# Nine of eleven feed-forward parts projected down by threes, as seven block products in place of eight

## The chip, the cores and the metric

The kernel runs on one core of a Trainium2 chip. Times are device microseconds of one execution, and the number that counts is their median. A core has TensorE (matrix products, written PE in the profile, its weight loads PEld), VectorE (DVE), ScalarE (ACT), GpSimd (POOL) and SyncE (SP), which here issues the loads. TensorE writes only to PSUM, eight banks of 512 fp32 columns; VectorE and ScalarE read and write PSUM, GpSimd does not.

## The reference, cut to what matters

Two sequences of 256 and 512 tokens go through a network of two layers, each a mixer and a feed-forward stage, with a normalisation before each. Weights are shared, and the kernel takes the two sequences side by side as 768 columns. The stage that is changed is this one, in both layers:

```python
def conv_ffn(h, w_up, conv_w, conv_b, w_down):
    u = h @ w_up                                  # 1024 -> 2 x 2816
    u = conv_general_dilated(u, conv_w, ...) + conv_b   # width 3, along the tokens
    g = u[..., :D_FF]
    val = u[..., D_FF:]
    return (jax.nn.silu(g) * val) @ w_down        # 2816 -> 1024
x = x + g2 * conv_ffn(h, ...)
```

All arrays are fp32. The kernel computes a product of two fp32 matrices with three products of the short type fp32r: each operand is split into a high part and a remainder (high x high, high x low, low x high).

## The kernel before, in words

Channels lie on the 128 partitions and tokens along the free axis, so that x is kept as eight channel chunks of 768 tokens, in two large tiles (`xt`).

The 2816 inner channels are cut into eleven parts of 256, that is two chunks of 128 for the gate and two for the value. `ffn` (L1372) loops over the parts. For each part `up` (L1405) makes:

- two calls of `pair` (L1194), one for the gate and one for the value. A pair is itself a block product by seven: input channel halves, two output chunks and token halves (384 columns) are combined, and `quarters` (L1162) issues twelve matmuls of 128x384 for each of the seven, into four fixed PSUM banks. Its weight blocks are summed on GpSimd (L1202 to L1214), split, and its sums are carried between banks by ScalarE copies (L1218, L1229);
- `conv` (L1384) on each chunk: one ScalarE and two VectorE instructions (L1387 to L1390);
- `silu` on ScalarE, put off into the next pair, and `product` (L1399): gate times value on GpSimd (L1402), then the split into high and low by `fp_copy_split` (L256), whose first line runs on ScalarE (L260) and whose second on VectorE (L261).

`down` (L1441) projects a finished part, while the loop is already at the next one. Its weights come in two loads of 128x1024, each split whole. Then for each output chunk c of eight and each sequence (512 and 256 tokens) it issues two times three matmuls into a PSUM bank of the group called `pa`, of four, and `resid` (L587) adds the result, times a factor, to x on VectorE. A part has 96 such matmuls and 16 such adds.

What sets the order: instructions are traced in program order, and a planner orders those of each engine by priority (earlier in the program first) and by its own estimate of when each is ready, and it inserts the waits. Where a block stands under `manual_schedule` with an engine's name, that engine keeps the program's order there. Outside, the matmuls of a part's down projection are laid between those of the next part's pairs. Each engine then executes its own list strictly in order. All loads go through the queue of SP, in order.

Buffers are handed out by name, and a new tile waits until an old one is no longer read. Those that matter:

```python
def slab(self, shape, dt=F32):   # tag "slab", bufs=6   (large, 12 KB a partition)
def tmp(self, shape, dt=F32):    # tag "nt",   bufs=8   (128x384)
def raw(self, src):              # tag "raw",  bufs=5   (a load, 128x1024)
def split(self, src):            # tags "whi", "wlo", bufs=3 each
```

In the feed-forward stage x holds two slabs, `urows` two (the first only in part 0), and the convolved rows `yrow` and the split product `g` take turns in the rest.

The last two parts, 9 and 10, are followed by the next stage's normalisation; part 0 is started by `head` (L1257), which is written out by hand and overlaps the end of the projection before.

Of the kernel before, what the change touches and what calls it, by code (L numbers as in the profile page):

```python
# [12 lines left out]
R = mybir.dt.float32r  # L13
# [3 lines left out]
P = 128  # L17
# [15 lines left out]
FF = 2816  # L33
FC = FF // P
NPART = FC // 2
EPS = 1e-6
LAG = 3

# [129 lines left out]
class Net:  # L168
# [1025 lines left out]
    def pair(self, pool, u, bank, rows, rest=False, behind=None):  # L1194
# [49 lines left out]
        self.quarters(d, part(wb, 1), self.T4, False)  # L1244
        self.evict(r2, d)

    def prepare(self, u0):
# [124 lines left out]
    def ffn(self, l, xt, pool, last_tile, apply, keep=None):  # L1372
# [22 lines left out]
        def silu(yrow):  # L1395
            for j in range(2):
                nc.scalar.activation(yrow[:, j], yrow[:, j], AF.Silu)

        def product(yrow, g):  # L1399
            for j in range(2):  # L1400
                y = yrow[:, 2 + j]
                nc.gpsimd.tensor_tensor(y, y, yrow[:, j], ALU.mult)  # L1402
                self.fp_copy_split(g[:, 0, j], g[:, 1, j], y)

        def up(p):  # L1405
# [8 lines left out]
            g = self.slab([P, 2, 2, TG], R)  # L1414
            for i in range(2):
                if p:
                    rows = [urow[:, 2 * i + j] for j in range(2)]
                    with ExitStack() as order:
                        for ins in behind[2 * i :] if p == 1 else ():
                            order.enter_context(self.tc.issue_after(ins))  # L1420

                        other = p == i == 1
                        bank = lambda j: self.pa()[:, :H] if j == 1 and other else fixed(j)
                        self.pair(pool, u0 + 3 * p + i, bank, rows, p == 1, held.pop() if held else None)
                for j in range(2):
                    conv(urow[:, 2 * i + j], yrow[:, 2 * i + j], i * FC + 2 * p + j)
                if i == 0:
                    held.append(lambda: silu(yrow))
            if p:
                product(yrow, g)  # L1430
            else:
                gate = held.pop()
                held.append(lambda: (gate(), product(yrow, g)))
            return g

        def mark(t):
# [231 lines left out]
```

## Time and profile before

| | |
|---|---|
| median of 3 runs | 1843.68 us (1842.69 to 1843.8) |
| the profiled execution | 1843.78 us, span 1842.0 us |
| TensorE | 1793.2 us busy, 97% of the span, 11290 matmuls |
| VectorE | 1367.0 us, 74% |
| ScalarE | 895.3 us, 49% |
| GpSimd | 488.0 us, 26% |
| granted clock of TensorE | 0.994 in the mean |
| the feed-forward parts in the steady state | 46.4 us each, TensorE busy throughout |

In the tables a line names the kernel's line, the engine, the operation, the tiles (written <- read), the shape and the count; behind the bar stand busy time and the mean duration of one in ns, then the idle time of the engine just before them and what ended it. The tables by stretch give for each window its length, then busy time and count for TensorE, its weight loads, VectorE, ScalarE and GpSimd, then the granted clock (1.00 is full), the DMA engines' share and GB/s. Rows of the timeline give start, duration and the instruction. Matmuls overlap one another, so that the distance of two starts is the time that one takes, not its own duration.

### The profile page before, as it was taken

The page shows a single profiled execution, that of the slowest core. Times are in us where ns is not written, and L with a number is a line of the kernel's source. Part 1 is how long each engine was busy: PE and PEld are TensorE (multiplying, and loading weights), DVE is VectorE, ACT ScalarE, POOL GpSimd, SP SyncE. Part 2 cuts the span into 40 slices and gives each one's busy share as a digit, 9 for nine tenths or more (in the row PEclk, how much of TensorE's full clock was granted, in tenths as well). Part 3 has the DMA queues.
Part 4 walks back from the last instruction along what each step waited for, and adds up shares of the span by engine and source line. Part 5 has one row for each costly group of instructions (what it writes and reads, how often), then busy time and mean ns, then how long its engine had stood idle before and what let it go on. Part 6 is the DMA issues. An engine that isn't in the chain of part 4 may idle for free.

```text
span 1842.0 us, 28931 instructions
## 1 busy us (share of the span) xinstructions
PE 1793.2 (97%) x11290; PEld 1657.4 (90%) x11290; DVE 1367.0 (74%) x2101; ACT 895.3 (49%) x1815; POOL 488.0 (26%) x386
## 2 busy tenths in 40 slices
PE   6999999999999999999999999999999999999997
PEld 3987887889998999999999999889989999999997
DVE  4755676886689877777777757766898777777776
ACT  4443443354456444444444556765564444444443
POOL 1001001021024333333331313430144333333322
PEclk9999999999999999999999999999999999999999
DMA  8344566546312221222223321124122222222212
GB/s 330 119 145 134 172 195 221 164 138 219 101 46 74 76 61 66 69 69 69 69 69 93 104 83 50 53 94 129 50 86 69 69 69 69 69 69 70 69 35 69
DMA packets 64245, 184.48 MB, mean 100 GB/s; under 512 B 6167, under 2 KB 23831, under 8 KB 64108
## 3 DMA queue, kind: packets, MB, share of 16 engines
q1 hardware_dynamic: 64108, 182.63, 30.8%
q8 instruction: 89, 1.46, 0.3%
q14 instruction: 48, 0.39, 0.1%
HBM read 176.17 MB, written 6.43 MB: 99 GB/s over the span
## 4 chain that ended last, share of the span: by engine, by line
PE 86%; DVE 6%; DMA 3%; ACT 2%; issue 1%; POOL 1%; SPq 0%; POOLq 0%; ACTq 0%; DVEq 0%
PE ps L254 27%; PE pa L254 25%; PE ps L1169 10%; PE ps L1172 10%; PE ps L1170 10%; PE pa L1008 1%; DMA slab<-in_adaln_w_dram 1%; DMA raw<-in_w_dram 1%; DVE wlo L261 1%; DVE ada L506 1%; DVE slab L590 1%; DMA raw<-in_adaln_w_dram 0%; PE pa L1172 0%; PE pa L1169 0%; PE pa L1170 0%
## 5 line engine op out<-in xcount | busy, mean ns | idle before, releaser
L260 ACT CAST whi<-raw 128x1024 fp32r<-128x1024 f32 x237 | 247.9, 1048 | 350.4 <-PE pa L254 161.4
L261 DVE TENSOR_TENSOR wlo<-raw,whi 128x1024 fp32r<-128x1024 f32 x237 | 316.6, 1337 | 119.8 <-ACT whi L260 117.3
L254 PE MATMUL pa<-slab,whi 128*128 128x256 f32 (+1 forms) x1472 | 346.6, 331 | 3.2 <-DVE slab L590 3.2
L254 PEld LDWEIGHTS pa<-slab,whi 128*128 128x128 f32 x1472 | 252.7, 188 | 27.5 <-DVE slab L590 4.5
L590 DVE SCALAR_TENSOR_TENSOR slab<-pa,mod,slab 128x256 f32<-128x256 f32 (+1 forms) x368 | 211.2, 592 | 70.8 <-PE pa L254 70.5
L254 PE MATMUL pa<-slab,wlo 128*128 128x256 f32 (+1 forms) x736 | 233.9, 330 | 0.0
L254 PE MATMUL ps<-zh,whi 128*128 128x256 f32 (+1 forms) x560 | 189.0, 339 | 2.3 <-ACT whi L260 1.7
L254 PE MATMUL ps<-zh,wlo 128*128 128x256 f32 (+1 forms) x560 | 184.1, 330 | 2.0 <-DVE wlo L261 2.0
L254 PE MATMUL ps<-zl,whi 128*128 128x256 f32 (+1 forms) x560 | 185.1, 332 | 0.0
L1169 PE MATMUL ps<-zh,whi 128*128 128x384 f32 x504 | 172.3, 342 | 3.6 <-ACT nt L1240 1.8
L1170 PE MATMUL ps<-zl,whi 128*128 128x384 f32 x504 | 169.9, 337 | 0.8 <-DVE zl L1126 0.8
L1172 PE MATMUL ps<-zh,wlo 128*128 128x384 f32 x504 | 168.9, 335 | 0.0
L254 PEld LDWEIGHTS pa<-slab,wlo 128*128 128x128 f32 x736 | 138.5, 188 | 13.1 <-DVE wlo L261 0.4
L1205 POOL TENSOR_TENSOR raw<-raw,raw 128x512 f32<-128x512 f32 x40 | 52.2, 1305 | 330.8 <-DVE wlo L261 259.4
L254 PE MATMUL ps<-slab,whi 128*128 128x384 f32 x512 | 132.0, 339 | 0.9 <-DVE slab L261 0.5
L1402 POOL TENSOR_TENSOR slab<-slab 128x772 f32<-128x772 f32 x44 | 86.5, 1967 | 164.6 <-DVE slab L1390 152.7
L1389 DVE SCALAR_TENSOR_TENSOR slab<-slab,cstt,slab 128x771 f32<-128x771 f32 x88 | 103.6, 1179 | 26.6 <-ACT slab L1387 26.5
L254 PEld LDWEIGHTS ps<-zh,whi 128*128 128x128 f32 x560 | 107.4, 192 | 15.9 <-issue 4.4
L506 DVE SCALAR_TENSOR_TENSOR ada<-raw,silc,ada 128x1024 f32<-128x1024 f32 x84 | 110.6, 1354 | 14.9 <-DMA raw<-in_adaln_w_dram 14.8
L1202 POOL TENSOR_TENSOR raw<-raw 128x512 f32<-128x512 f32 x40 | 68.5, 1712 | 200.1 <-DMA raw<-in_w_dram 169.7
L254 PEld LDWEIGHTS ps<-zh,wlo 128*128 128x128 f32 x560 | 107.2, 192 | 12.2 <-DVE wlo L261 2.9
L254 PEld LDWEIGHTS ps<-zl,whi 128*128 128x128 f32 x560 | 107.4, 192 | 11.9 <-issue 3.4
(291 smaller groups left out, 4265.7 us busy)
## 6 DMA issues: line engine op xcount, KB each, us to landing
raw<-in_w_dram SPq DMA_DIRECT2D x208, 512.0 KB, 3.7
raw<-in_adaln_w_dram SPq DMA_DIRECT2D x84, 512.0 KB, 4.6
slab<-in_x_dram SPq DMA_DIRECT2D x12, 512.0 KB, 6.8
slab<-in_adaln_w_dram SPq DMA_DIRECT2D x12, 512.0 KB, 10.3
slab<-mrows SPq DMA_DIRECT2D x8, 384.0 KB, 5.3
xs<-slab SPq DMA_DIRECT2D x6, 512.0 KB, 3.6
bt<-brow SPq DMA_DIRECT2D x16, 192.0 KB, 3.0
slab<-xs SPq DMA_DIRECT2D x6, 512.0 KB, 6.9
```

The lines of the kernel that those rows point to most:

```text
L254: self.nc.tensor.matmul(out, lhsT, rhs, start=start, stop=stop)
L260: nc.scalar.copy(hi, src)
L261: return nc.vector.tensor_tensor(lo, src, hi.bitcast(F32), ALU.subtract)
L506: stt(acc[:, s], row, w, acc[:, s], ALU.mult, ALU.add)
L590: self.nc.vector.scalar_tensor_tensor(x, o, self.mod[l][:, gc + c, q : q + 1], x, ALU.mult, ALU.add)
L1169: mm(o, wh[:, k], hi[k], start=start and k == 0, stop=False, skip_group_check=True)
L1170: mm(o, wh[:, k], lo[k], start=False, stop=False, skip_group_check=True)
L1172: mm(o, wl[:, k], hi[k], start=False, stop=k == 3, skip_group_check=True)
L1202: tt(q[2], q[2], q[3], ALU.add)
L1205: tt(q[0], q[2], q[0], ALU.subtract)
L1389: stt(y[:, 1:], u[:, :-1], w(0), y[:, 1:], ALU.mult, ALU.add)
L1402: nc.gpsimd.tensor_tensor(y, y, yrow[:, j], ALU.mult)
```

## The change

Parts 0 to 8 are no longer projected down one by one. Their products of gate and value stay unsplit in two slabs, `kept`: two parts of a group of three in one, the third in another, whose end also takes one load of weights. When the first pair of part 3, 6 or 9 has been traced, `blocked` projects the three parts before it at once.

It cuts the output channels into halves (four chunks each), each part's inner channels into its two chunks, and the tokens into halves of 384. A 2x2 by 2x2 block product then takes seven products of blocks in place of eight. The sums of weight blocks are made on GpSimd, those of product blocks on VectorE, both in place between the uses; each of the seven products splits its three weight blocks (128x512) and its three product blocks (128x384), `ready(i)`, one step ahead of its matmuls. A step is 36 matmuls of 384 columns, into four banks: X are the `pa` banks, Y the fixed ones that the pairs use too. Between steps ScalarE copies a partial sum from one set of banks to the other, four copies, and `resid` adds finished blocks to x: 32 adds a group. TensorE is under `manual_schedule` inside each step.

The order of the tiles within a step is either part 0 for all four chunks and then parts 1 and 2, or parts 0 and 1 and then part 2.

Parts 9 and 10 are projected as before.

```diff
+WHOLE = 9
...
+    def blocked(self, l, xt, units, ys, more):
+        gp, tt = nc.gpsimd.tensor_tensor, nc.vector.tensor_tensor
+        ra = [self.load(u, 0) for u in units]
+        rb = [self.load(u, 1) for u in units[:2]] + [more]
+        nc.sync.dma_start(more, self.io["w"][units[2], :, 1024:2048])
...
+        for p in each:
+            gp(a21[p], a21[p], a22[p], ALU.add)
+        for p in each:
+            tt(b12[p], b22[p], b12[p], ALU.subtract)
+
+        stream = [(a11, b11), (a12, b21), (a11, b11), (a12, b22), (a11, b12), (a21, b11), (a22, b21)]
...
+        def ready(i):
+            for p in each:
+                n = 3 * i + p
+                if n % 2 == 0:
+                    whole[:] = [self.stg.tile([P, 1024], R, tag=t, name=self.nm(t), bufs=3) for t in ("whi", "wlo")]
+                w = [half(t, n % 2) for t in whole]
+                y = [self.tmp([P, H], R) for _ in range(2)]
+                self.fp_copy_split(*w, stream[i][0][p])
+                self.fp_copy_split(*y, stream[i][1][p])
+                parts[n] = w, y
+            for p in each:
+                if i == 0:
+                    gp(a11[p], a21[p], a11[p], ALU.subtract)
+                    tt(b11[p], b11[p], b12[p], ALU.add)
+                elif i == 1:
+                    gp(a12[p], a12[p], a11[p], ALU.subtract)
+                    tt(b21[p], b21[p], b11[p], ALU.subtract)
+                elif i == 2:
+                    gp(a11[p], a22[p], a11[p], ALU.subtract)
+                    tt(b11[p], b22[p], b11[p], ALU.subtract)
+
+        X = [self.pa()[:, :H] for _ in range(4)]
+        Y = [self.bank[c][:, :H] for c in range(4)]
...
+        last_two = [(c, 0) for c in range(4)] + [(c, p) for c in range(4) for p in (1, 2)]
+        first_two = [(c, p) for c in range(4) for p in (0, 1)] + [(c, 2) for c in range(4)]
+        steps = [
+            (X, last_two, True, lambda c: nc.scalar.copy(Y[c], X[c])),
+            (X, first_two, False, lambda c: add(c, 0, X[c])),
+            (Y, last_two, False, lambda c: nc.scalar.copy(X[c], Y[c])),
+            (Y, first_two, False, lambda c: add(c, H, Y[c])),
+            (X, last_two, False, lambda c: add(c + 4, H, X[c])),
+            (Y, last_two, True, lambda c: (add(c, H, Y[c]), add(c + 4, H, Y[c]))),
+            (X, last_two, False, lambda c: add(c + 4, 0, X[c])),
+        ]
+        ready(0)
+        ready(1)
+        for i, (o, order, start, done) in enumerate(steps):
+            if i:
+                ready(i + 1)
+            with self.tc.manual_schedule(engines={mybir.EngineType.PE}):
+                for c, p in order:
...
+                    mm(o[c], wh[:, cs], yh, start=start and p == 0, stop=False, skip_group_check=True)
+                    mm(o[c], wh[:, cs], yl, start=False, stop=False, skip_group_check=True)
+                    mm(o[c], wl[:, cs], yh, start=False, stop=p == 2, skip_group_check=True)
+                    if p == 2:
+                        done(c)
...
-        def product(yrow, g):
+        def product(yrow, p, g):
             for j in range(2):
                 y = yrow[:, 2 + j]
+                if g is None:
+                    for p0, p1, _ in pieces(0, T):
+                        b = slice(col(p0), col(p0) + p1 - p0)
+                        nc.gpsimd.tensor_tensor(place(p)[:, j, p0:p1], y[:, b], yrow[:, j, b], ALU.mult)
+                    continue
...
+                    if p and p % 3 == 0 and p <= WHOLE:
+                        ys = [place(p - 3 + z) for z in range(3)]
+                        self.blocked(l, xt, [u0 + 3 * (p - 3 + z) + 2 for z in range(3)], ys, kept[1][:, 2 * T :])
...
-            prev = (p, g)
+            prev = (p, g) if p >= WHOLE else None
```

More of the change, by code (lines that the diff above doesn't have):

```diff
@@ L1397, in silu, with place @@
                 nc.scalar.activation(yrow[:, j], yrow[:, j], AF.Silu)
-        def product(yrow, g):
+        def product(yrow, p, g):
             for j in range(2):
                 y = yrow[:, 2 + j]
+                if g is None:
[3 more added lines that the diff above has]
+                    continue
                 nc.gpsimd.tensor_tensor(y, y, yrow[:, j], ALU.mult)
                 self.fp_copy_split(g[:, 0, j], g[:, 1, j], y)
+        kept = []
+        def place(p):
+            if p % 3 < 2:
+                if not kept:
+                    kept.append(self.slab([P, 2, 2, T]))
+                return kept[0][:, p % 3]
+            if len(kept) < 2:
+                kept.append(self.slab([P, 2 * T + 1024]))
+            return kept[1][:, : 2 * T].rearrange("p (j t) -> p j t", j=2)
         def up(p):
@@ L1413, in up @@
             yrow = self.slab([P, 4, TG])
-            g = self.slab([P, 2, 2, TG], R)
+            g = self.slab([P, 2, 2, TG], R) if p >= WHOLE else None
             for i in range(2):
@@ L1428, in up @@
                     held.append(lambda: silu(yrow))
+                    if p and p % 3 == 0 and p <= WHOLE:
+                        ys = [place(p - 3 + z) for z in range(3)]
+                        self.blocked(l, xt, [u0 + 3 * (p - 3 + z) + 2 for z in range(3)], ys, kept[1][:, 2 * T :])
             if p:
-                product(yrow, g)
+                product(yrow, p, g)
             else:
                 gate = held.pop()
-                held.append(lambda: (gate(), product(yrow, g)))
+                held.append(lambda: (gate(), product(yrow, p, g)))
             return g
```

15 lines of the change are left out of this document (added).

## The prediction

> **What bounds the kernel now.** I read the page first, then tables by stretch over the feed-forward stage, then the groups by shape, then the timeline of one part.
>
> ```profile
> span 1842.0 us, 28931 instructions
> PE 1793.2 (97%) x11290; PEld 1657.4 (90%) x11290; DVE 1367.0 (74%) x2101; ACT 895.3 (49%) x1815; POOL 488.0 (26%) x386
> ```
> ```profile
> core 0: us, PE busy (x) PEld busy (x) DVE busy (x) ACT busy (x) POOL busy (x), PEclk, DMA share, GB/s
> 545.00:570.00 25.00, 22.88 (x124) 21.43 (x125) 24.86 (x25) 17.95 (x29) 12.54 (x6) 1.00 0.29 89
> 570.00:600.00 30.00, 28.64 (x157) 26.10 (x156) 28.66 (x30) 16.50 (x25) 14.22 (x7) 1.00 0.23 71
> ...
> 669.90:809.16 139.26, 139.26 (x793) 132.02 (x793) 105.71 (x120) 64.35 (x103) 50.95 (x30) 1.00 0.22 69
> ```
>
> The last row is three parts in the steady state: TensorE is never idle in 139.26 us at full granted clock, VectorE works 76% of it, GpSimd 37%. One part is 139.26 / 3 = 46.42 us. So a matmul taken away there shortens the kernel, as long as its place is not taken by a wait. The two rows above are the beginning of the first layer's feed-forward stage: there VectorE is full (24.86 of 25, 28.66 of 30) and TensorE already has holes.
>
> ```profile
> 793.62 0.33 PE L1169 MATMUL ps<-zh,whi 128*128 128x384 f32 x1
> ...
> 802.58 0.34 PE L1170 MATMUL ps<-zl,whi 128*128 128x384 f32 x1
> ```
>
> These rows lie in a stretch of one projection pair with no other matmuls. From the first start to the last are 51 steps in 8.96 us: 0.1757 us for each 384-wide matmul. The 0.33 or 0.34 is latency; matmuls overlap.
>
> **Matmuls.** A part has two pairs of 84 matmuls: 168 x 0.1757 = 29.5 us. Its down projection is the rest: 46.42 - 29.5 = 16.9 us, 50.7 us for three parts. The new block has 7 steps x 12 (tile, part) pairs x 3 = 252 matmuls of 384: 252 x 0.1757 = 44.3 us, a step 6.33 us. Saved: 6.45 us a group, six groups (three in each layer), 38.7 us. That is all there is to gain.
>
> **VectorE, ScalarE and GpSimd in a group.** Durations, all from groups by shape:
>
> ```profile
> L261 DVE TENSOR_TENSOR wlo<-raw,whi 128x1024 fp32r<-128x1024 f32 x237 | 316.6, 1337 | 119.8 <-ACT whi L260 117.3
> L261 DVE TENSOR_TENSOR slab<-slab,slab 128x772 fp32r<-128x772 f32 x44 | 53.1, 1207 | 0.0
> L590 DVE SCALAR_TENSOR_TENSOR slab<-pa,mod,slab 128x512 f32<-128x512 f32 x160 | 116.5, 742 | 26.4 <-PE pa L254 26.4
> L590 DVE SCALAR_TENSOR_TENSOR slab<-pa,mod,slab 128x256 f32<-128x256 f32 x208 | 95.2, 477 | 44.4 <-PE pa L254 44.1
> L590 DVE SCALAR_TENSOR_TENSOR slab<-ps,mod,slab 128x384 f32<-128x384 f32 x16 | 9.8, 613 | 16.8 <-PE ps L254 16.8
> L590 DVE SCALAR_TENSOR_TENSOR slab<-ps,mod,slab 128x128 f32<-128x128 f32 x16 | 5.6, 347 | 19.8 <-PE ps L254 19.8
> L261 DVE TENSOR_TENSOR s1l<-raw,s1h 128x512 fp32r<-128x512 f32 x40 | 41.2, 1029 | 0.0
> L1126 DVE TENSOR_TENSOR zl<-bq,zh 128x384 fp32r<-128x384 f32 x24 | 13.3, 554 | 5.1 <-ACT zh L1120 4.9
> L260 ACT CAST s1h<-raw 128x512 fp32r<-128x512 f32 x40 | 24.6, 616 | 3.9 <-PE ps L1170 3.7
> L1120 ACT CAST zh<-bq 128x384 fp32r<-128x384 f32 x24 | 12.2, 516 | 12.1 <-DVE bq L1130 11.0 <-DVE bq L1143 1.1
> L1229 ACT COPY ps<-ps 128x384 f32<-128x384 f32 x40 | 18.8, 471 | 26.9 <-PE ps L1172 26.9
> L1205 POOL TENSOR_TENSOR raw<-raw,raw 128x512 f32<-128x512 f32 x40 | 52.2, 1305 | 330.8 <-DVE wlo L261 259.4
> ```
>
> And how VectorE and GpSimd slow each other, from the timeline of one part, first VectorE's rows, then GpSimd's:
>
> ```profile
> 764.80 1.02 DVE L1389 SCALAR_TENSOR_TENSOR slab<-slab,cstt,slab 128x771 f32<-128x771 f32 x1
> 770.54 1.61 DVE L1389 SCALAR_TENSOR_TENSOR slab<-slab,cstt,slab 128x771 f32<-128x771 f32 x1
> 772.74 1.38 DVE L261 TENSOR_TENSOR slab<-slab,slab 128x772 fp32r<-128x772 f32 x1
> 774.71 1.39 DVE L1390 SCALAR_TENSOR_TENSOR slab<-slab,cstt,slab 128x771 f32<-128x771 f32 x1
> 776.02 1.26 DVE L590 SCALAR_TENSOR_TENSOR slab<-pa,mod,slab 128x256 f32<-128x256 f32 x3
> 777.27 1.37 DVE L261 TENSOR_TENSOR s1l<-raw,s1h 128x512 fp32r<-128x512 f32 x1
> 779.00 0.96 DVE L261 TENSOR_TENSOR slab<-slab,slab 128x772 fp32r<-128x772 f32 x1
> 803.38 0.69 DVE L261 TENSOR_TENSOR s1l<-raw,s1h 128x512 fp32r<-128x512 f32 x1
> ```
> ```profile
> 770.04 1.30 POOL L1205 TENSOR_TENSOR raw<-raw,raw 128x512 f32<-128x512 f32 x1 [1.16 <-DVE wlo L261]
> 771.42 1.89 POOL L1206 TENSOR_TENSOR raw<-raw 128x512 f32<-128x512 f32 x1
> 773.26 2.02 POOL L1214 TENSOR_TENSOR raw<-raw,raw 128x512 f32<-128x512 f32 x1
> 776.24 1.85 POOL L1402 TENSOR_TENSOR slab<-slab 128x772 f32<-128x772 f32 x1 [0.96 <-DVE slab L1390]
> ```
>
> While GpSimd worked from 770.04 to 778.1, four VectorE operations with two SBUF inputs took 1.61, 1.38, 1.39 and 1.37 instead of 1.02, 0.96, 1.02 and 0.69: 2.06 us more for four GpSimd operations, 0.5 us each. The adds out of PSUM (three in 1.26) did not slow. The Trainium skill's GPSIMD Engine Reference, section Key points, says the same: GpSimd shares its SBUF interfaces with VectorE, and contends with VectorE instructions that have two SBUF inputs. That speaks against this change, which trades adds out of PSUM for splits of that kind; the page has no size for it, so by the page alone VectorE's sum below would stay without its term for GpSimd.
>
> VectorE, a group: removed are 48 adds (24 x 0.742 + 24 x 0.477 = 29.3), six weight splits (8.0) and six splits of the product (7.2): 44.5 us. Added are 21 weight splits (0.69 alone, 1.03 mean: 14.5 to 21.6), 21 splits of the product at 0.554 (11.6), 12 sums of blocks (the same shape, 6.6), and 16 adds of 384, 8 of 256, 8 of 128 (9.8 + 3.8 + 2.8 = 16.4): 49 to 56 us. So VectorE stands at 110 to 117 of 132.8 us: it does not bound the group as a whole. ScalarE, a step: 3 x 0.616 + 3 x 0.516 + 4 x 0.471 = 5.3 of 6.33 us, hidden. GpSimd, a group: 12 sums of weight blocks at 1.3 to 1.9 (16 to 23 us), and four pieces of the product in place of two (at most 5.2 for 3.9 a part): 70 to 78 of 133 us, hidden.
>
> **The block itself is where it is tight.** Put 0 at the block's first matmul. The buffers decide when splits can be made: three weight slots hold six (product, part) halves, and eight small tiles hold four pairs of the moving operand. The pair in front gives up its second weight slot after its sixth quarter (12 matmuls, 2.1 us each: -2.1 us), its small tiles at about the same time, its last slot at 0. Of step 0 only parts 0 and 1 can be ready ahead; from -2.1 on everything else is made beside the matmuls. The last deadline is part 2 of step 6, at 6 x 6.33 + 2.6 = 40.6 us. In these 42.7 us VectorE has: the pair's two last sums 1.1; its convolution, which the program names first, 4 x 1.02 = 4.1; 19 weight splits x 0.69 = 13.1; 18 others x 0.554 = 10.0; 9 sums of blocks 5.0; the adds of steps 1, 3, 4 and half of 5 (3.3 + 2.45 + 2.45 + 2.45 = 10.7); the next pair's first split and s1 (1.2 + 0.69 = 1.9): 45.9. Neighbours overlap a little (three 256-wide adds in 1.26, not 1.43: 0.06 each), 66 operations, so 41.9. Some 11 GpSimd operations fall inside (six to eight block sums, four sums of the next pair) x 0.5: 47.4. That is 4.7 us too much; 4.35 of it (the half of step 5 and the next pair) may slip behind the deadline, which leaves 0.4. TensorE's late time per group lies between these, and I take 3.0, because VectorE works in order, each split waits for ScalarE's half first, and step 1 is due soonest (convolution, third parts of step 0, two parts of step 1: 10 us of work in 9). Ends for the range: 0, and 9 if all 12 block sums, the next pair's four and the four pieces of a product fall inside (20 x 0.5 in place of 5.5) and nothing slips. Six groups: 18 us, 0 to 54.
>
> Loads: the block takes all five buffers, so the second pair's two loads wait for the fifth product's splits, at about 20 us of 44.3; landing, GpSimd's sums and three splits need 3.7 + 5 + 4 us. Covered; if not, the third quarter of that pair is late. One tile for the convolved rows in place of two: the product must be done before the next convolution, 7 us against 14.8 of the next pair. Hidden.
>
> ```profile
> raw<-in_w_dram SPq DMA_DIRECT2D x208, 512.0 KB, 3.7
> ```
>
> **The loss of filling work in part 1.** Down tiles of part 0 ran between the quarters of part 1's pairs:
>
> ```profile
> 574.75 2.80 PE pa L254 x12
> ...
> 585.24 3.53 PE pa L254 x24
> 590.85 2.10 PE pa L254 x12
> 595.07 4.17 PE pa L254 x18
> ```
>
> These are 66 matmuls, 11.6 us, in a time when VectorE is full. They go to the block. VectorE loses there the split of product 0 (2 x 1.2), half of the part's 16 adds (4 x 0.742 + 4 x 0.477 = 4.9) and one of its weight splits (1.3): 8.6 us. TensorE gets 3 us of new waiting in each layer, 6 us; ends 0 (the holes hide in what is late anyway) and 23 (nothing fills).
>
> **Sum.** The profiled execution took 1843.78 us, span 1842.0 and 1.8 around it; the median is 0.1 below. 1843.8 - 38.7 + 18 + 6 = 1829 us.
>
> **The rivals.** First: the waits stay hidden, because the order of tiles in the steps (part 0 first, or part 2 last) gives every split two thirds of a step; for it speaks the steady state, where TensorE never waited for a split. 1843.8 - 38.7 + 0 to 12 = 1805 to 1817. Second, on the other side: VectorE becomes the bound of the block. It decides from (38.7 - 6) / 6 = 5.5 us a group on; half way from there to 9, at 7.3, it is 1843.8 - 38.7 + 44 + 6 = 1855. For it speaks the 47.4 above before any latency, against it that half the adds can slip. Third: the clock.
>
> ```profile
> 37.00:40.00 3.00, 2.56 (x18) 2.25 (x18) 3.00 (x11) 3.00 (x11) 0.00 (x0) 0.96 1.03 412
> 40.00:43.00 3.00, 3.00 (x15) 3.00 (x16) 3.00 (x11) 3.00 (x8) 0.00 (x0) 0.50 0.44 176
> 43.00:46.00 3.00, 3.00 (x16) 3.00 (x15) 3.00 (x7) 1.96 (x5) 0.00 (x0) 0.50 0.00 0
> ```
>
> After a row of tiny matmuls the granted clock was 0.50 for 6 us, which costs 3 us of work. If the 3 us of each group came in one piece and did this, it adds 18: 1847. But in the stretch from 545, where TensorE had 2.1 us of holes, the clock stayed at 1.00. The Trainium skill's TensorE: Matmul & The Clock Gate, Part 1, has the rule: an idle window of about 3.4 us halves the clock; the row at 40 agrees with the half.
>
> **Chances.** My forecast, with 1817 to 1840: 0.37. Hidden: 0.25. Waits that just eat the gain, within 0.2% (3.7 us, about what a measurement of this kernel can tell): 0.10. VectorE the bound: 0.25. The clock: 0.03. So faster 0.62, same 0.10, slower 0.28. The range 1805 to 1857 leaves out only the far ends; the likeliest case's own is 1817 to 1840.
>
> **What would show it.** Right: 216 matmuls fewer, about 44 to 48 us from a block's first matmul to its last, waits of TensorE for split results (lines 260 and 261) at the second and third step, VectorE over 90% in the block, new holes around 575 to 600 us. Wrong: blocks of 44.3 us without a hole (first rival), or of 51 and more (second), or a hole behind the block at the next pair, where I see cover; a granted clock below 1.00 there is the third.

## The result, and the profile after

| | median | runs | to before |
|---|---|---|---|
| before | 1843.74 us | 4 runs, 1842.69 to 1845.46 | |
| changed | 1901.93 us | 4 runs, 1898.83 to 1903.16 | 1.0312 [1.0294, 1.033] |

The change makes the kernel 3.1% slower, 58 us, where 1829 was predicted; the time lies 45 us above the range. In the changed kernel lines 36 to 1242 of before have a number one higher (the split's second half is L262 in place of L261); the block's matmuls are L1321 to L1323.

From the page of the changed kernel, its span, TensorE, VectorE and GpSimd, and the shares of the chain that ended last:

```profile
span 1900.0 us, 29305 instructions
...
PE 1785.8 (94%) x11074; PEld 1673.8 (88%) x11074; DVE 1455.9 (77%) x2257; ACT 975.9 (51%) x2043; POOL 627.4 (33%) x494
...
PE 60%; DVE 21%; POOL 6%; issue 5%; DMA 5%; ACT 4%; SPq 0%; POOLq 0%; ACTq 0%
```

The same row of the chain before:

```profile
PE 86%; DVE 6%; DMA 3%; ACT 2%; issue 1%; POOL 1%; SPq 0%; POOLq 0%; ACTq 0%; DVEq 0%
```

The 216 matmuls are gone (11290 to 11074), but TensorE is busy only 7.4 us less, and its idle time has grown from 48.8 us (1842.0 - 1793.2) to 114.2. Time has gone from TensorE to VectorE and GpSimd: their shares of the chain are 21% and 6% in place of 6% and 1%. What TensorE waits for, from the waits of the changed kernel (what waits, for what: us in total, times, longest):

```profile
PE pa L1322 <- DVE nt L262: 30.3, 10, 4.7
PE ps L1170 <- ACT ps L1219: 22.3, 20, 2.3
PE ps L1322 <- DVE nt L262: 11.5, 7, 2.2
...
PE ps L1170 <- ACT nt L1241: 4.3, 2, 2.2
PE pa L1323 <- DVE wlo L262: 3.8, 6, 0.6
```

Two places, then. The three rows of L1322 and L1323 (45.6 us) are the block waiting for VectorE's half of a split. The two L1170 rows (26.6 us) are the pairs waiting for copies on ScalarE, most of all the copy at the head of a pair (L1219). By stretch, in the changed kernel: the block of the first group, the pairs up to the next block, the second block, and two windows inside it:

```profile
626.40:684.52 58.12, 50.28 (x267) 48.44 (x267) 56.61 (x87) 25.48 (x51) 21.27 (x14) 0.94 0.17 55
684.52:775.44 90.92, 86.77 (x491) 85.70 (x491) 63.64 (x61) 52.91 (x90) 52.77 (x36) 1.00 0.22 70
775.44:834.23 58.79, 51.05 (x268) 49.01 (x268) 55.49 (x87) 25.06 (x50) 21.94 (x14) 0.94 0.15 54
783.00:789.00 6.00, 1.30 (x8) 0.98 (x7) 6.00 (x7) 2.64 (x6) 3.28 (x3) 1.00 0.00 0
789.00:792.00 3.00, 3.00 (x11) 3.00 (x12) 3.00 (x5) 0.00 (x0) 0.00 (x0) 0.56 0.02 5
```

A block with 14 matmuls of the next pair between is 266 x 0.1757 = 46.7 us of work, and it takes 58.5 in the mean of these two: 11.7 us lost. VectorE works 56.61 of 58.12 us and 55.49 of 58.79. The 490 matmuls of pairs between are 86.1 us of work and take 90.9: 4.8 lost. And after a hole in which TensorE works 1.30 of 6 us the granted clock drops to 0.56.

What VectorE does in that hole, from the timeline of the second block, VectorE first, then GpSimd, then TensorE:

```profile
778.22 0.54 DVE L262 TENSOR_TENSOR nt<-slab,nt 128x384 fp32r<-128x384 f32 x1
778.69 0.55 DVE L1285 TENSOR_TENSOR slab<-slab 128x384 f32<-128x384 f32 x1
...
780.36 1.64 DVE L262 TENSOR_TENSOR nt<-slab,nt 128x384 fp32r<-128x384 f32 x1
781.93 1.65 DVE L1285 TENSOR_TENSOR slab<-slab 128x384 f32<-128x384 f32 x1
783.50 1.01 DVE L1469 SCALAR_TENSOR_TENSOR slab<-slab,cstt,slab 128x771 f32<-128x771 f32 x1
...
785.63 1.61 DVE L1288 TENSOR_TENSOR slab<-slab 128x384 f32<-128x384 f32 x1
787.17 1.61 DVE L262 TENSOR_TENSOR nt<-slab,nt 128x384 fp32r<-128x384 f32 x1
```
```profile
779.91 1.68 POOL L1284 TENSOR_TENSOR raw<-slab,raw 128x512 f32<-128x512 f32 x1 [2.97 <-DVE wlo L262]
781.55 1.61 POOL L1287 TENSOR_TENSOR raw<-raw 128x512 f32<-128x512 f32 x1
785.25 3.12 POOL L1287 TENSOR_TENSOR raw<-raw 128x512 f32<-128x512 f32 x2 [2.09 <-DVE wlo L262]
```
```profile
788.84 0.44 PE L1322 MATMUL pa<-nt,whi 128*128 128x384 f32 x1 [4.70 <-DVE nt L262]
...
791.49 0.52 PE L1322 MATMUL pa<-nt,whi 128*128 128x384 f32 x1
791.81 0.52 PE L1323 MATMUL pa<-nt,wlo 128*128 128x384 f32 x1
```

The same instruction of VectorE, two inputs of 128x384 out of SBUF, takes 0.54 us alone and 1.6 beside a GpSimd sum. Four were hit, and they meet four sums: the first ends at 782.00, 0.41 after its sum (781.59), the second at 783.58, 0.42 after (783.16), the fourth at 788.78, 0.41 after (788.37). Each looks as if it began its real work only when the GpSimd sum was through. The split at 787.17 is the one TensorE waits for, 4.70 us; after that the matmuls start 0.32 us apart in place of 0.1757.

In the pairs, ScalarE's rows show a cast of the second weight load, which waits 0.92 us for GpSimd's sum, and behind it the copy; TensorE's row is the matmul that waits for the copy:

```profile
717.99 1.05 ACT L261 CAST whi<-raw 128x1024 fp32r<-128x1024 f32 x1 [0.92 <-POOL raw L1215]
718.94 0.53 ACT L1183 COPY slab<-ps 128x128 f32<-128x128 f32 x2
719.37 0.49 ACT L1219 COPY ps<-ps 128x384 f32<-128x384 f32 x1
```
```profile
719.91 0.44 PE L1170 MATMUL ps<-zh,whi 128*128 128x384 f32 x1 [1.60 <-ACT ps L1219]
```

### The profile page after: what moved, and what is told of

It is laid out like the page before. It is cut to its first block, busy times and chain, and to the rows that moved or that the text cites. A ratio compares the mean times of both kernels' runs of the same rounds, so it can differ in the third digit from the quotient of the medians.

```text
span 1900.0 us, 29305 instructions
## 1 busy us (share of the span) xinstructions
PE 1785.8 (94%) x11074; PEld 1673.8 (88%) x11074; DVE 1455.9 (77%) x2257; ACT 975.9 (51%) x2043; POOL 627.4 (33%) x494
## 4 chain that ended last, share of the span: by engine, by line
PE 60%; DVE 21%; POOL 6%; issue 5%; DMA 5%; ACT 4%; SPq 0%; POOLq 0%; ACTq 0%
PE ps L255 26%; PE pa L255 9%; DVE wlo L262 6%; PE ps L1170 5%; PE ps L1171 5%; PE ps L1173 5%; DVE nt L262 3%; DVE slab L591 3%; DMA raw<-in_w_dram 2%; DVE slab L1469 2%; DVE slab L1470 2%; ACT whi L261 2%; POOL raw L1206 2%; POOL raw L1207 1%; PE pa L1009 1%
## 5 line engine op out<-in xcount | busy, mean ns | idle before, releaser
L262 DVE TENSOR_TENSOR wlo<-raw,whi 128x1024 fp32r<-128x1024 f32 (+1 forms) x315 | 361.5, 1158 | 103.6 <-ACT whi L261 102.6
L261 ACT CAST whi<-raw 128x1024 fp32r<-128x1024 f32 (+1 forms) x315 | 275.3, 892 | 189.3 <-PE ps L1171 49.2
L1170 PE MATMUL ps<-zh,whi 128*128 128x384 f32 x504 | 172.4, 342 | 26.7 <-ACT ps L1219 22.3
L1173 PE MATMUL ps<-zh,wlo 128*128 128x384 f32 x504 | 169.7, 337 | 0.0
L1469 DVE SCALAR_TENSOR_TENSOR slab<-slab,cstt,slab 128x771 f32<-128x771 f32 x88 | 120.3, 1369 | 36.6 <-ACT slab L1467 36.6
L1467 ACT ACTIVATE slab<-slab,cstt 128x772 f32<-128x772 f32 x88 | 91.2, 1037 | 98.2 <-DVE slab L1243 97.8
L1322 PE MATMUL pa<-nt,whi 128*128 128x384 f32 x288 | 104.5, 363 | 30.9 <-DVE nt L262 30.3
L1485 POOL TENSOR_TENSOR slab<-slab 128x512 f32<-128x512 f32 x72 | 107.4, 1512 | 67.4 <-DVE slab L1470 50.3
L1170 PEld LDWEIGHTS ps<-zh,whi 128*128 128x128 f32 x504 | 95.3, 189 | 34.5 <-ACT ps L1219 29.4
L255 PEld LDWEIGHTS ps<-zh,whi 128*128 128x128 f32 x560 | 106.6, 191 | 15.3 <-issue 4.4
L261 ACT CAST nt<-slab 128x384 fp32r<-128x384 f32 x126 | 63.6, 515 | 108.2 <-PE pa L1322 70.4
L262 DVE TENSOR_TENSOR nt<-slab,nt 128x384 fp32r<-128x384 f32 x126 | 100.5, 805 | 10.4 <-ACT nt L261 10.4
L1323 PE MATMUL pa<-nt,wlo 128*128 128x384 f32 x288 | 102.4, 355 | 3.8 <-DVE wlo L262 3.8
```

The lines of the kernel that those rows point to most:

```text
L255: self.nc.tensor.matmul(out, lhsT, rhs, start=start, stop=stop)
L261: nc.scalar.copy(hi, src)
L262: return nc.vector.tensor_tensor(lo, src, hi.bitcast(F32), ALU.subtract)
L1170: mm(o, wh[:, k], hi[k], start=start and k == 0, stop=False, skip_group_check=True)
L1173: mm(o, wl[:, k], hi[k], start=False, stop=k == 3, skip_group_check=True)
L1322: mm(o[c], wh[:, cs], yl, start=False, stop=False, skip_group_check=True)
```

## The experiments

Theory after the result: the loss has two parts, VectorE late in the block because GpSimd's 12 weight sums slow its splits (about 70 us), and the pairs, which have lost the down projection's matmuls between them and now wait for ScalarE (about 30 us). Rivals: the planner's order of VectorE's work; the slow clock after each stall; the pairs shifted by the blocks. Diffs are against the changed kernel unless said otherwise.

**1. The sums left out.**

```diff
-        gp, tt = nc.gpsimd.tensor_tensor, nc.vector.tensor_tensor
+        gp, tt = lambda *a: None, nc.vector.tensor_tensor
```

> The twelve sums of weight blocks of each group on GpSimd are left out (a11, a12 and a21 are used as loaded), so the output is not the reference's; the matmuls, splits, loads and VectorE's sums all stay. Theory (VectorE's two-input splits run at 1.6 us in place of 0.55 while GpSimd adds weights, which fills VectorE in the first steps of the block, and the stall of 4.7 us there also halves the clock): the long stall goes or falls under 2 us, the clock stays at 1.00 in the block, a block takes 47 to 51 us in place of 58, and the time is 1840 to 1870 us. Rival (the number of VectorE's operations and the slots are what is late, whoever runs beside them): the block stays at 55 us or more, 1885 us or more.

Measured: 1830.07 us (1828.25 to 1831.09), 0.9924 [0.9893, 0.9956] of before. VectorE and the first block of this run, and two of its groups by shape (count, busy time, mean ns):

```profile
PE 1761.7 (96%) x11074; PEld 1659.7 (91%) x11074; DVE 1387.6 (76%) x2257; ACT 976.1 (53%) x2043; POOL 507.1 (28%) x422
```
```profile
626.16:672.61 46.45, 46.41 (x267) 46.09 (x267) 44.62 (x82) 24.67 (x51) 6.97 (x6) 1.00 0.21 69
```
```profile
L262 DVE TENSOR_TENSOR nt<-slab,nt 128x384 fp32r<-128x384 f32 x126 | 68.6, 552 | 9.3 <-ACT nt L261 9.3
```

The changed kernel's row of the same group:

```profile
L262 DVE TENSOR_TENSOR nt<-slab,nt 128x384 fp32r<-128x384 f32 x126 | 100.5, 805 | 10.4 <-ACT nt L261 10.4
```

The block runs without a hole at its 46.5 us, and 71.9 us are back (1901.93 - 1830.07). The 72 sums on GpSimd cost VectorE 1455.9 - 1387.6 = 68.3 us of busy time, 0.95 us each. This run alone does not tell contention from the wait for the sums themselves; the sixth does.

**2. The convolution traced after the block.** The call of `blocked` is put ahead of the loop over `conv` in `up`, to take the convolution's passes out of the block's head.

> The block is traced ahead of the convolution of the first pair's rows, so that the block's splits come first on VectorE and ScalarE; nothing is left out. Theory (VectorE's order in the first 15 us of the block decides): the 4.7 us stall loses the 1 us of convolution that lies before it, the later stalls lose up to 3 us, the clock may still halve: 1875 to 1895 us. If the stall falls under 3.4 us and the clock stays up: 1865 us. Rival (the slots decide, not the order): within 4 us of 1902.

Measured: 1900.84 us (1899.46 to 1902.21). The planner wrote the same order for VectorE as before the edit, and the stall of 4.7 us stayed. So this run tested nothing; the thirteenth forces the order.

**3. and 5. Small matmuls in the stalls.** Matmuls of 128 columns into an unused part of a bank, to keep TensorE busy where it waits (the diff is the third run's; the fifth has (1, 1), (2, 4) and 40, 20):

```diff
+                    if (i, z) in ((1, 8), (2, 4)):
+                        hi, _ = self.quarter(self.B11)
+                        for _ in range((44, 20)[i - 1]):
+                            mm(self.bank[3][:, H:], hi[0][:, :P], hi[0][:, :P], start=False, stop=False, ...)
```

> 44 matmuls of 128 columns, which nothing reads, are put ahead of the third parts in the second step and 20 ahead of the second part in the third step, where the stalls are. They add no output and keep TensorE active while it waits. Theory (after the stall the clock is granted at half for about 4 us): the clock stays at 1.00 in the block, and a block loses 3 to 4 us of its 58: 1880 to 1890 us. If the low clock costs nothing by itself, since VectorE is the bound behind it: 1900 us or a little more, with the stalls longer by what the matmuls gain.

> As the dummy matmuls of before, but now put where the traces show the stalls: 40 ahead of the second tile of the second step (its part 1 waits 4.7 us there), 20 ahead of part 1 in the third step. One takes 0.114 us, so 40 fill 4.6 us and 20 fill 2.3. Theory (the low clock after the 4.7 us stall costs about 3.5 us a block by itself): the granted clock stays at 1.00 in the block and a block takes 54 to 55 us in place of 58, time 1878 to 1888 us. Rival (VectorE is behind all along, so that what the low clock costs is waiting anyway): later waits grow by as much, within 5 us of 1902.

Measured: 1928.94 us (1924.91 to 1932.97) and 1912.23 (1907.26 to 1917.19). The third run's 44 stood behind the stall and not in it. The fifth run's stood in it, but 40 took 7.7 us, longer than the stall, and the matmuls after them still started 0.32 us apart. The granted clock had fallen to 0.50 during the small matmuls (6 us from 637.0 in the first block), though the wait ahead of them was of 1.35 us only. The third run's 44, which followed full-size matmuls without a wait, ran 4.8 us at 1.00. So small matmuls held the clock in one run and not in the other, and what it goes by these runs do not settle. In the slower one of the fifth's two executions TensorE also waits 9.4 us for a load, outside the blocks. Neither run separates the clock's share; the twelfth does.

**4. The blocks left out**, so that only the pairs remain of parts 0 to 8.

```diff
-                        self.blocked(l, xt, ...)
+                        0 and self.blocked(l, xt, ...)
```

> The blocks are left out, so parts 0 to 8 are not projected down at all and the output is not the reference's; pairs, convolution, products and parts 9 and 10 stay. Kernel before less six groups of 50.7 us of down projection is 1539 us if the pairs never wait without filling work. Theory (pairs alone lose about 4 to 5 us in each three parts to ScalarE's copy between banks, and 3 us at part 1): 1555 to 1570 us. Rival (all of the loss is in the blocks): 1537 to 1545 us.

Measured: 1570.07 us (1568.39 to 1571.75). Without a loss it would be 1843.7 - 38.7 - 1512 x 0.1757 = 1539.3. The wait of the changed kernel for the copy at a pair's head is there, nearly whole (22.1 us against 22.3):

```profile
PE ps L1170 <- ACT ps L1219: 22.1, 19, 2.2
```

So the pairs by themselves lose 31 us, with no block and no block's sum near them. With the blocks' 6 x 11.7 = 70 this accounts for the result: 1843.7 - 38.7 + 70 + 31 = 1906 against 1901.9.

**6. The weight sums on VectorE.**

```diff
-        gp, tt = nc.gpsimd.tensor_tensor, nc.vector.tensor_tensor
+        gp = tt = nc.vector.tensor_tensor
```

> The twelve sums of weight blocks of a group move from GpSimd to VectorE: the same dependencies, 12 x 0.69 = 8.3 us more work for VectorE in each group, and no GpSimd beside it in the block. Theory (what is lost is VectorE's contention with GpSimd): VectorE gets 8.3 us more and loses some 9 us of stretching in the block, so the 4.7 us stall goes or halves and the clock stays up: 1850 to 1880 us. Rival (the sums come too late on GpSimd as a dependency, or VectorE is simply short of time): with more work on VectorE 1900 us or more.

Measured: 1866.81 us (1864.78 to 1871.34), 1.0125 [1.0109, 1.0141] of before: 35 us faster than the changed kernel.

```profile
PE 1771.5 (95%) x11074; PEld 1662.1 (89%) x11074; DVE 1435.8 (77%) x2329; ACT 977.8 (52%) x2043; POOL 506.1 (27%) x422
```

VectorE executes 72 instructions more and is busy 20 us less (1435.8 against 1455.9). A sum that GpSimd takes off VectorE costs VectorE more, 0.95 us, than making it itself, 0.67 ((1435.8 - 1387.6) / 72). That is contention: the time is VectorE's own busy time, and not idle time before a split, so a wait for a late sum does not explain it.

**7. to 9. The copy ahead of the waiting split.** In the seventh run the copy was traced earlier and under high priority, in the eighth with the sums on VectorE besides; the ninth forces it:

```diff
-        wb = self.split(rb)
         e, b = bank(1), bank(2)
-        nc.scalar.copy(b, fork)
+        ahead = nc.scalar.copy(b, fork)
+        with self.tc.issue_after(ahead.ins):
+            wb = self.split(rb)
```

> In each pair the ScalarE copy that opens the second bank (line 1219 of the changed kernel) is traced ahead of the splits of s1 and of the last two weight tiles, and with priority. Theory (pairs without filling work lose 1.2 to 2.2 us in each part because that copy stands behind a split that waits for GpSimd): TensorE's waits for this copy, 22 us in all in the changed kernel, go to under 8: 1880 to 1890 us. Rival (the copy is late because its input or bank is late): waits stay, within 4 us of 1902.

> The sums of weight blocks on VectorE and the copy first, together. If both theories hold the two gains add up: 1830 to 1865 us, the lower end beats the kernel before. If only the contention holds it is as the one with the sums alone.

> Edit: in pair() the split of the second half-unit (wb) is issued on ScalarE only after the fork copy, forced this time; the blocks and GpSimd's sums are as in the changed kernel. Theory (the pairs' own part of the loss is ScalarE's queue: the copy stands behind a split that waits for GpSimd's sum): TensorE's waits for the fork copy fall from 22.3 us in 10 stretches to under 8, the block's stalls of 4.7 and 2 us stay, time 1882 to 1890. Rival (the copy is late for another reason, the evictions ahead of it or the same contention, or the split is then late in its turn): waits of the same sum move to the quarters that read wb, time 1898 to 1906.

Measured: 1904.4 us (1902.8 to 1905.99), 1866.88 (1863.31 to 1868.44) and 1896.38 (1893.05 to 1900.27). In the seventh and eighth the planner kept the copy where it was, except in part 1 (its waits are 22.9 us in the seventh), so they say nothing on it; the eighth repeats the sixth. In the ninth the order changed:

```profile
PE ps L1170 <- ACT ps L1218: 9.4, 9, 2.6
```

Of 22.3 us of waits 12.9 went, not quite to the "under 8" that was expected, and the time fell by 5.5 us only, not by the 12 to 20 written down. The pairs' stretch is 88.65 us in place of 90.92; the first block, 60.60 in place of 58.12, gave back what one stretch won. Over the whole trace the four stretches between two blocks are 9.3 us shorter in sum, and the six blocks are 4.2 us longer. Another 3.6 us are new waits of the pairs for the split that now comes behind the copy (L1173 for `wlo`), as the rival had it. So theory and rival each hold in part.

**10. and 11. Both edits, and VectorE's third sums later.** The tenth is the sixth with the ninth's order. The eleventh also moves `tt(b21[p], b21[p], b11[p], ...)` from `i == 1` to `i == 2`, behind the third product's splits.

> Edit: the forced order of the copy and, in addition, the blocks' weight sums on VectorE. Theory (two causes that add: contention in the block, ScalarE's queue in the pairs): 1866.8 us of the run with sums on VectorE alone, less the 15 to 20 us of the copy's waits, so 1843 to 1852. Rival (the copy's wait and the block's stalls feed each other, and the one goes with the other): 1862 to 1868, with the copy's waits already gone in the run with sums on VectorE alone or moved elsewhere.

> Edit: as the kernel with both edits, and the third sum of the second product's activations (b21 less b11) is written behind the third product's splits, so that VectorE serves the splits that TensorE waits for first. Theory (what is left in the block is the order of VectorE's work and not its amount): the 2.56 us stall at the step boundary falls under 1 us in each of the 6 blocks, time 9 to 15 us below the kernel with both edits, 1832 to 1842. Rival (VectorE's amount of work is the bound of the block): the stall moves to a later product by the same sum, time within 3 us of the kernel with both edits.

Measured: 1866.24 us (1865.2 to 1867.18) and 1866.83 (1860.3 to 1869.07). In the tenth the theory's number missed and the rival's came. The copy's waits fell from the sixth's 19.0 us to 8.9, but the block's longest stall grew from 2.6 to 3.1: the four stretches of pairs between two blocks are 8.4 us shorter in sum than in the sixth, and the six blocks 9.7 us longer. What the pairs won, the blocks gave back; why their stalls grew was not tested. The eleventh tested nothing: VectorE executes the same 2329 instructions in the same order as in the tenth, so the planner had not moved the sums, and the same stall of 3.1 us says nothing on them.

**12. Matmuls of full size in the stalls.** Repeats of the block's own matmuls:

```diff
+                    for _ in range({(1, 0, 1): 27, (2, 0, 2): 12}.get((i, c, p), 0)):
+                        mm(o[c], wh[:, cs], yh, start=False, stop=False, skip_group_check=True)
```

> Edit: the changed kernel with 39 more 384-wide matmuls in each block, repeats of the block's own products: 27 ahead of the matmul at which TensorE stalls 4.7 us, 12 ahead of the one at which it stalls 2 to 2.2 us (they are added into the sums, so the result is left wrong by these repeats; no VectorE work is added). At 0.1757 us they take 4.7 and 2.1 us, about what the stalls last. Theory (the slow clock after a stall is a cost of its own, some 3.7 us a block): the stalls are filled, the granted clock stays 1.00 in the block, and the time falls by 6 x 3.7 = 22 us for nothing but more matmuls: 1877 to 1886. Rival (the matmuls are slow for another reason, contention or operands, and the clock row only goes with it): no gain, 1900 to 1915.

Measured: 1901.34 us (1899.25 to 1902.95). Its first two blocks:

```profile
624.48:682.97 58.49, 54.78 (x307) 52.65 (x306) 56.28 (x87) 25.45 (x51) 21.89 (x15) 1.00 0.17 55
774.81:832.33 57.52, 54.54 (x307) 52.70 (x306) 54.90 (x86) 24.96 (x50) 22.23 (x14) 1.00 0.16 56
```

My theory here fell. The clock stayed at 1.00, as it said, but the gain did not come: 39 matmuls more in each block, 6.9 us of work, and a block lasts as long as without them (58.12 and 58.79). What the clock gives back, TensorE waits for elsewhere (1.5 and 0.6 us at the third step), since VectorE delivers no earlier. The slow clock is real and costs next to nothing here: 0.6 us in the whole time (1.0302 of before against 1.0312), less than the runs scatter.

**13. and 14. The block's head in order.** On top of the tenth, the convolution's four passes are held behind the third product's splits:

```diff
-                    conv(urow[:, 2 * i + j], yrow[:, 2 * i + j], i * FC + 2 * p + j)
...
+                    if block:
+                        order.enter_context(self.tc.issue_after(self.gate.ins))
+                    for j in range(2):
+                        conv(urow[:, 2 * i + j], yrow[:, 2 * i + j], i * FC + 2 * p + j)
```

`self.gate` is the last split of `ready(2)`, and `blocked` is traced first. The fourteenth also puts `ready` under `manual_schedule` for ScalarE and VectorE.

> Edit: sums on VectorE and the copy ahead of the split, and the convolution that stood in the head of the block (4 passes of 1.02 us on VectorE) issued only after the third product's splits, forced this time. Theory (order at the head of the block: VectorE works there without a hole, so 4 us taken out of it bring every later split 4 us forward): the stalls of 1.6 and 3.1 us shrink to under 1 us together, the clock stays up, 4 to 6 us a block, 1830 to 1843. Rival (VectorE's whole amount bounds the block): the passes only come back later as another stall, 1860 to 1868.

> Edit: as the run with the convolution behind the splits, and inside the block ScalarE and VectorE keep the program's order, so that the third product's splits stand ahead of the sums of the fourth. Theory (order): no stall over 1 us is left up to the third product, 1826 to 1840, at or below the kernel before. Rival (amount): the fourth product's splits are late instead, within 4 us of the run before it.

Measured: 1850.75 us (1845.52 to 1852.75, 10 runs), 1.0024 [1.0013, 1.0035] of before, and 1855.97 (1851.66 to 1863.0), 1.0057 [1.0035, 1.0078]. The thirteenth's first block and its first 30 us:

```profile
624.62:676.26 51.64, 47.96 (x267) 45.85 (x267) 51.64 (x96) 25.68 (x51) 7.23 (x5) 1.00 0.19 62
624.62:655.00 30.38, 27.12 (x149) 25.32 (x149) 30.38 (x59) 17.86 (x38) 0.00 (x0) 1.00 0.04 7
```

The order was worth 15 us against the tenth: no stall is over 1.2 us and the clock is 1.00. Now VectorE is busy for 51.64 of 51.64 us: it bounds the block. Why the fourteenth is 5 us slower the traces do not show; its block is as long (51.5 us).

**15. No sums, and the copy first.**

> Edit: the 12 weight sums of each group left out (their blocks are used unsummed, so the result is not the reference's) and the copy ahead of the split. Theory (the copy's waits are a loss of the pairs alone, and independent of the blocks): 1830 of the run without sums less some 5 to 12 us, 1818 to 1825. Rival (the waits only come because the blocks shift the pairs' work): unchanged, 1828 to 1832.

The edit is the first run's with the ninth's. Measured: 1824.41 us (1821.33 to 1826.74), 0.9881 [0.9865, 0.9897] of before. As the theory said, 5.7 us below the first run, with no block's sum anywhere: the copy's place is a loss of the pairs' own. This is how much the seven block products would bring with this order if their weight sums were free: 1.2%. Of the waits for the copy (19.1 us in the first run), half are still there, two of 2.6 us in part 1:

```profile
PE ps L1170 <- ACT ps L1218: 10.3, 11, 2.6
```

**16. to 18. Amount against order.** On top of the thirteenth: the three first sums (a21 with a22) back on GpSimd, ahead of the block; the convolution behind the fourth product's splits (`i == 3`); both.

```diff
-            gp(a21[p], a21[p], a22[p], ALU.add)
+            nc.gpsimd.tensor_tensor(a21[p], a21[p], a22[p], ALU.add)
...
-                if i == 2 and p == 2:
+                if i == 3 and p == 2:
```

> Edit: as the run with the convolution behind the third product's splits, and the three first sums of weights (a21 and a22) back on GpSimd, where they run during the pairs ahead of the block; the nine others stay on VectorE. Theory (amount): 2 us of VectorE's work per group leave the head of the block, and the stalls shrink by about as much, 6 to 12 us in all: 1838 to 1845. Rival (GpSimd's sums slow VectorE's work in the pairs by more than they take off): 1850 to 1860.

> Edit: as the run with the convolution behind the third product's splits, but behind those of the fourth. Theory (order): two passes of 1.03 us leave the stretch in which the fourth product's splits are made, the two stalls of 0.8 us at them go, 5 to 10 us in all: 1840 to 1846. Rival (amount, VectorE has no slack in any of the first four products): within 3 us of that run, 1848 to 1854.

> Edit: both of the two before. Theory: their gains add, 1832 to 1842, faster than the kernel before by 0.1 to 0.6%. Rival: no better than the better of the two.

Measured: 1857.54 us (1855.78 to 1863.18), 1854.83 (1853.03 to 1856.76) and 1862.83 (1860.91 to 1864.91). The rival's number came in the first; the second lies just above its rival's range (1848 to 1854), far from the theory's; the third is worse than either. The first block of the seventeenth:

```profile
625.05:677.34 52.29, 47.96 (x267) 45.83 (x267) 52.29 (x96) 25.68 (x51) 6.89 (x5) 1.00 0.19 61
```

VectorE is full to the last microsecond again; the convolution's passes moved later make a stall of 1.3 to 1.6 us at the fifth product in place of one of 0.8 at the fourth. The three sums a group on GpSimd cost 7 us more than they take off, even beside the pairs. Contention is one part of it: with 18 sums fewer VectorE is busy only 2.2 us less (1425.9 against 1428.1). GpSimd's own queue may be another: VectorE's wait for the products of gate and value, among which the sums now stand, grew from 20.0 to 27.7 us. No variant with the whole result beats the kernel before. For the thirteenth the account nearly closes: 1843.7 - 38.7, plus six blocks at 51.6 in place of 46.7 (30), plus six stretches of pairs at 88.1 in place of 86.1 (12), is 1847, between the profiled execution (1845.52) and the median (1850.75).

## Why the prediction was wrong

**Matmuls.** Right: 216 fewer, 0.1757 us each, and a block without its sums takes 46.45 us against 46.7 computed. The 38.7 us of matmuls are gone; the fifteenth run, with the weight sums left out, keeps 22 us of them.

**VectorE, ScalarE and GpSimd in a group: the term for GpSimd was mis-sized.** I read "0.5 us each" from rows in which VectorE's operation began with 0.6 to 0.8 us of GpSimd's left (770.54 against an end at 771.34, 774.71 against 775.28). In the block VectorE has its next operation ready at once and meets each sum near its beginning, with 1.2 us left (780.36 against 781.59). Each weight sum cost 0.95. With 12 of them in place of "some 11" that is 11.4 us where I had 5.5, and VectorE's demand up to the last deadline goes from 47.4 to 53.3 against 42.7: 10.6 us too much, near the 11.7 that were lost. I quoted a page of the Trainium skill that says that the two engines contend, and said that it has no size for it. Another page of the Trainium skill gives the kind, which I passed over: Trainium Architecture — The Big Picture, section What this means for kernel authors, calls the shared pair of ports an exclusive lock and not a bandwidth split. The trace agrees in its times: a 384-wide split ended 0.4 us behind the sum it met, and so took 1.6 us in place of 0.54. By a lock, the price of a meeting is what is left of GpSimd's instruction, whatever VectorE's own length; the runs are in line with that, but none tested it by itself.

**The block itself.** The forecast of 3.0 us a group was the failing step: 11.7 were lost. Whether the 4.35 slipped behind the last deadline no run shows. The sum weighed the work mainly against that deadline, and the stalls came early, at the second and third step (4.7 and some 2 us): the planner's order kept the convolution ahead of the splits there, worth 15 us of the whole kernel in the thirteenth run, where the sums are on VectorE. The second rival, VectorE the bound of the block, is what happened, and its point of decision (5.5 us a group) was passed; at 11.7 its own formula gives 1843.8 - 38.7 + 70 + 6 = 1881. My ends, 0 and 9, did not reach it.

**The change's other end: "a hole behind the block at the next pair, where I see cover".** Wrong, and the part that no rival held. I looked at the loads there, and no load stands in the chain that leads to the wait behind the first block (at 688.58, 2.15 us). What came was ScalarE: once no down projection stands between the quarters, a pair of 84 matmuls has nothing to fill the time in which the copy at its head is queued behind a cast that waits for GpSimd. I had put a part's pairs at 29.5 us from a stretch of one pair of before, and took that for all. The pairs lose 31 us by themselves, of which the term "lost filler in part 1" had 6. Putting the copy ahead of the cast gave 5.5 and 5.7 us of it back (ninth and fifteenth runs); the rest stays, 1824.4 - 1805 = 19 us in the fifteenth, 10.3 of them as waits for the same copy. What makes it late then is open. The chain further on, in the changed kernel, has more links than ScalarE's queue: VectorE frees a buffer with a split (719.97), the load into it takes 4.76 us, three sums on GpSimd follow (726.03 to 730.50), and then the cast. No run separates them. The term for part 1 asked the right question at one part of eleven, and it belonged to all nine.

**The clock.** The third rival's hole came in every block (4.7 us in one piece, then 0.56 granted), at the 0.03 I gave it; the price of 18 us did not come, since the twelfth run took the slow clock away and gained nothing. Shorter waits were enough too: behind one of 2.24 us in the changed kernel's second block (at 801.51) the clock was 0.60 from 804 to 807, and behind the sixth run's of 2.57 us it fell in three of six blocks.

```profile
804.00:807.00 3.00, 3.00 (x13) 3.00 (x11) 2.49 (x6) 1.66 (x4) 0.00 (x0) 0.60 0.00 0
```

The rule that I quoted, an idle window of about 3.4 us in the Trainium skill's TensorE: Matmul & The Clock Gate, Part 1, agrees with the hole of 4.70 us and not with these; here the measurement decides.

**What would show it.** VectorE over 90% in the block (97 and 94%), waits for the splits at the second and third step: as written. Blocks of 51 us and more, the mark of the second rival: 58. The new holes around 575 to 600 us did not come: from 570 to 600 TensorE works 29.67 of 30 us, before 28.64.

## What to carry to other kernels

Work that is moved to GpSimd is not free because GpSimd is idle: where VectorE has two SBUF inputs, price each meeting by what is left of the GpSimd instruction (here 0.95 us for a sum of some 1.6), and compare with making it on VectorE. When a stage's matmuls shrink, list every wait that those matmuls used to cover, on each engine in turn, ScalarE's queue too, in all the parts and not only in the one where the cover is thin already. And an engine that is 76% busy over a stage may be the bound of the one stretch into which the change packs its work; sum its work against that stretch's length first.

## What the runs showed of the hardware

- A VectorE operation with two SBUF inputs of 128x384 fp32 takes 0.54 us alone and 1.6 beside a GpSimd sum of 128x512; the sum costs VectorE 0.95 us in the mean, more than the 0.67 of making it there.
- The granted clock fell to 0.56 behind a stall of 4.70 us, with matmuls 0.32 us apart in place of 0.1757, and to 0.60 behind one of 2.24. Forty matmuls of 128 columns behind a wait of 1.35 us did not prevent it, 27 of 384 columns did; 44 of 128 columns right behind full-size ones ran at 1.00.
- In these blocks, where VectorE delivers the operands late, the slow clock hides: with it and without it a block takes 58 us (58.12 and 58.79 against 58.49 and 57.52).
